# A two-layer attention encoder on one Trainium2 core: the first layer's value products regrouped, and the last gate columns cut unevenly

## The chip, the cores and the metric

The kernel runs on one core of one Trainium2 chip. The metric is the device time of one execution in microseconds (us). Before the change the median of three executions is 668.27 us (667.93 to 668.65).

The engines are named as the profile names them: PE is TensorE (PEld its weight loads), DVE is VectorE, ACT is ScalarE, POOL is GpSimd, SP is SyncE, whose queue issues most DMAs.

## The reference

Two layers over 512 tokens of 1024 features, batch 1. Layer 0 mixes tokens by a two-dimensional neighbourhood attention with 16 heads of 64 channels; layer 1 by a dense latent attention with rotary parts. Cut to what matters here:

```
def mixer_na(xn, w_in, rpb, w_out):                 # layer 0
    q, k, v, z = split(xn @ w_in, 4)                # 1024 columns each
    o = neighbourhood_attention(q, k, v, rpb)       # 16 heads; softmax over an 8 x 16 window
    return (o * silu(z)) @ w_out

def mixer_mla(xn, w_in, q_norm, w_qb, kv_norm, w_kvb, w_out):   # layer 1
    c_q, c_kv, k_rope, z = split(xn @ w_in)
    q, kv = rmsnorm(c_q) @ w_qb, rmsnorm(c_kv) @ w_kvb
    # the rotary part of q and k: x * cos + swapped(x) * sin
    return (attention(q, k, v) * silu(z)) @ w_out

for i in range(2):
    h = x + mixer[i](rmsnorm(x))
    gate = sigmoid(rmsnorm(h) @ ple_w_gate[i])
    x = h + gate * (p[i] @ ple_w_proj[i])
return rmsnorm(x)
```

## The kernel before

**Split products.** Every operand of a large product is held as two float32r tiles, `hi` (a rounded copy) and `lo` (the rest), and a product is three: hi·hi, lo·hi, hi·lo. `load_w` brings a block of weights (`wraw`, 128x1024) in by SP's queue, ACT rounds it to `whi` (L78) and POOL subtracts to `wlo` (L79). Each of the three has a ring of three buffers, so a block can be loaded only when the block three before it has been used up by PE.

**Order.** The kernel is written as a stream of tile operations; a scheduler in the build then sets the order on every engine by what its own timeline takes to be ready. Each engine runs its list strictly in that order. Buffers of a pool are handed out in the order in which the source asks for them. PSUM has eight banks: two named `mm` (projections), two `S` (scores), three `T` (transposed softmax weights), one `O` (a head's output).

**Layer 0's heads** (`na_heads`). Heads go in eight pairs. `values()` makes V of the first eight heads: 96 products of 512 columns into the three `T` banks and the `O` bank at once, ahead of all heads. `project(j)` makes a pair's queries and keys (two groups of 24 products of 512 columns in the `mm` banks). For j = 4 and j = 6 it first makes V of two further pairs (four heads): four groups of 24 products of only 256 columns each, in the `mm` banks. `attend(j)` runs the two heads of a pair; in the source `project(j + 1)` stands ahead of `attend(j)`.

**One head** (`na_head`). Four query quarters. Scores go to the two `S` banks, two quarters in each (L335, L336; 8 products). DVE adds the bias into the tile `ex` and takes the row maximum (L342 for the first quarter, in two pieces, L345 for the others; each with a short read of the accumulator). ACT takes the exponential (L352), DVE the reciprocal of the row sum (L354, once for two quarters), POOL multiplies (L358). PE transposes `ex` block by block into two `T` banks (L369, L371; 7 transposes, the third of the first bank needs the fourth quarter). ACT rounds to `ph` (L89), DVE subtracts to `pl` (L91); PE multiplies by V into the `O` bank (L383; 8 products, the last four need the second `T` bank's `ph` and `pl`). ACT and DVE bring the halves of O together (`half_of`, L193 and L194), POOL multiplies by the gate z (L198). `ex` has two buffers, so the maxima of a head can be written only when the head two before it is transposed.

**Layer 1's start** (`rope`). The rotary part of the queries goes ACT, DVE (shuffle L584, product with cos L585), POOL (product with sin L586, sum L587), ACT (L588), POOL (L589), and by DMA into the query tile `qe` of the first scores.

**The end** (`gate_phase`, `done`). The last output tile's 512 columns of the gate product are made in two groups of 24 products with 256 columns. Per group ACT takes the sigmoid (L480) and DVE applies it (L481, L483). For the first group ACT sums squares (L875) and DVE scales the sum (L876, tile `mn`); for the second DVE does that itself (L871) on top of the first's `mn`. Then POOL takes the root (L882), ACT and DVE scale the row (L886, L883, L885) and two DMAs write it.

Of the kernel before, what the change touches and what calls it, by code (L numbers as in the profile page):

```python
# [14 lines left out]
F32R = mybir.dt.float32r  # L15
AF = mybir.ActivationFunctionType
ALU = mybir.AluOpType
AX = mybir.AxisListType
PSUM = bass.MemoryType.PSUM
P = 128  # L20
S = 512
D = 1024
NT = S // P
KD = D // P
# [15 lines left out]
class Trunk:  # L40
# [172 lines left out]
    def na_heads(self, pool, xT, zs, oT):  # L213
        nc, a = self.nc, self.a
        xh, xl = xT
        X = lambda t, k, kt: t[k // 4][:, k % 4, kt * P:(kt + 1) * P]
        V, A, U = {}, {}, {}

        def values():

            pss = [self.psum(b) for b in ("T", "T", "T", "O")]
            for c in range(4):
                w = self.load_w(a["na_v0"][c], 1024)
                for i, (s, r) in enumerate(((0, 0), (1, 0), (0, 1))):
                    for kt, ps in enumerate(pss):
                        for k in (2 * c, 2 * c + 1):
                            nc.tensor.matmul(ps, X((xh, xl)[s], k, kt), w[r][:, k % 2 * S:(k % 2 + 1) * S],  # L227
                                             start=k == 0 and i == 0, stop=k == KD - 1 and i == 2)
            for g in range(2):
                V[g] = [pool.tile([P, S], F32R, name="vt", tag="vt", bufs=8) for kt in range(NT)]  # L230
            for kt, ps in enumerate(pss):
                for g in range(2):
                    self.v_split(V[g][kt], ps[:, g * 256:(g + 1) * 256])

        def project(j):
            if j in (4, 6):
                g = j // 2
                wv = [self.load_w(a["na_v1"][g - 2, c], 1024) for c in range(2)]
                vts = V[g] = []
                for kt in range(4):  # L240
                    ps = self.psum("mm")
                    W = lambda s, k: wv[k // 4][s][:, (k % 4) * 256:(k % 4 + 1) * 256]
                    t = [(X(xh, k, kt), W(0, k)) for k in range(KD)]
                    t += [(X(xl, k, kt), W(0, k)) for k in range(KD)]
                    t += [(X(xh, k, kt), W(1, k)) for k in range(KD)]
                    self.mms(ps[:, :256], t)
                    vt = pool.tile([P, S], F32R, name="vt", tag="vt", bufs=8)
                    self.v_split(vt, ps[:, :256])
                    vts.append(vt)
            wq = self.load_w(a["na_qk"][j], 1024)  # L250
            psq = self.psum("mm")
            self.proj_T(psq, wq, xT)
            sa = pool.tile([P, S], F32R, name="sa", tag="qs", bufs=4)
            sb = pool.tile([P, S], F32R, name="sb", tag="qs", bufs=4)
            nc.scalar.activation(sa[0:64], psq[0:64], AF.Copy, scale=0.125)
            nc.scalar.activation(sb[64:128], psq[64:128], AF.Copy, scale=0.125)
            nc.vector.scalar_tensor_tensor(sa[64:128], psq[0:64], 0.125, sa[0:64].bitcast(F32),
                                           op0=ALU.mult, op1=ALU.subtract)
            nc.vector.scalar_tensor_tensor(sb[0:64], psq[64:128], 0.125, sb[64:128].bitcast(F32),
                                           op0=ALU.mult, op1=ALU.subtract)  # L260
            s0 = []
            for s in (sa, sb):
                e0 = pool.tile([P, P], F32R, name="s0", tag="s0", bufs=4)
                nc.vector.tensor_copy(e0.rearrange("p (a b) -> p a b", a=2),
                                      win(s, 0, P, 0, [[448, 2], [1, 64]]).bitcast(F32))
                s0.append(e0)
            wk = self.load_w(a["na_qk"][8 + j], 1024)
            psk = self.psum("mm")
            last = self.proj_T(psk, wk, xT)
            da = pool.tile([P, S], F32R, name="da", tag="kd", bufs=4)  # L270
            db = pool.tile([P, S], F32R, name="db", tag="kd", bufs=4)
            la, lb = self.rest_k[j % 2]
            nc.scalar.activation(da[0:64], psk[0:64], AF.Copy)
            nc.scalar.activation(da[64:128], psk[0:64], AF.Copy)
            nc.scalar.activation(db[64:128], psk[64:128], AF.Copy)
            nc.scalar.activation(db[0:64], psk[64:128], AF.Copy)
            nc.vector.tensor_tensor(out=la[0:64], in0=psk[0:64], in1=da[0:64].bitcast(F32), op=ALU.subtract)
            nc.vector.tensor_tensor(out=lb[64:128], in0=psk[64:128], in1=db[64:128].bitcast(F32), op=ALU.subtract)
            A[j] = (sa, sb), s0, (da, db), (la, lb)
            return last  # L280

        def attend(j):
            sq, s0, dk, kl = A.pop(j)
            O = []
            for e in range(2):
                c = (2 * j + e) % 4 * P
                O.append(self.na_head(pool, 2 * j + e, sq[e], s0[e], dk[e], kl[e],
                                      [vt[:, c:c + P] for vt in V[j // 2]]))
            U[j] = self.combine(pool, O[0], O[1], 2 + NLATE)
            if j in zs:  # L290
                self.gated(U[j], zs[j], oT, j)


        self.rest_k = []
        for i in range(2):
            la = pool.tile([P, S], F32R, name=f"la{i}", bufs=1)
            lb = pool.tile([P, S], F32R, name=f"lb{i}", bufs=1)
            nc.gpsimd.memset(la[64:128].bitcast(F32), 0.0)
            nc.gpsimd.memset(lb[0:64].bitcast(F32), 0.0)
            self.rest_k.append((la, lb))  # L300
        values()
        last = project(0)
        for j in range(8):
            if j < 7:
                last = project(j + 1)
            attend(j)
        late = range(8 - NLATE, 8)
        zs.update(self.z_phase(a["na_z"], xT, late, self.last_exp.ins))
        for j in late:
            self.gated(U[j], zs[j], oT, j)  # L310
        return last.ins
# [153 lines left out]
    def gate_phase(self, pool, layer, hnT, rh, res, after):  # L465
        nc, a = self.nc, self.a
        for n in range(2):
            ws = [self.load_w(a["gate"][layer, n, c], 1024, extra=n == 1 or c == 3) for c in range(4)]
            for t in range(NT):
                pe = pool.tile([P, S], F32, name="pe", tag="pe", bufs=3)  # L470
                nc.sync.dma_start(pe, self.pe[layer][t][:, n * S:(n + 1) * S])
                last = layer == 1 and n == 1 and t == NT - 1
                w = S // 2 if last else S
                for o in range(0, S, w):
                    ps = self.psum("mm")[:, :w]
                    L = lambda s, k: hnT[t][:, s * KD + k, :]
                    W = lambda s, k: ws[k // 2][s][:, (k % 2) * S + o:(k % 2) * S + o + w]
                    self.mms(ps, self.by_chunk(L, W))
                    sg = pool.tile([P, S], F32, name="sg", tag="sg", bufs=2)[:, :w]
                    nc.scalar.activation(sg, ps, AF.Sigmoid, scale=rh[t])  # L480
                    nc.vector.tensor_tensor(out=sg, in0=pe[:, o:o + w], in1=sg, op=ALU.mult)  # L481
                    r = res[t][:, n * S + o:n * S + o + w]
                    nc.vector.tensor_tensor(out=r, in0=r, in1=sg, op=ALU.add)  # L483
                    after(t, n, o, w)
# [49 lines left out]
    def mla_heads(self, pool, xT, cT, sets, oT):  # L534


        nc, a = self.nc, self.a
# [6 lines left out]
        R, V, W_, A, PS = {}, {}, {}, {}, {}  # L544
# [31 lines left out]
        def rope(g, a0, a1):  # L576
# [6 lines left out]
            A["r", g] = nc.scalar.activation(xr, psr, AF.Copy)  # L583
            nc.vector.stream_shuffle(sw, xr, swap)  # L584
            nc.vector.tensor_tensor(out=xr, in0=psr, in1=rc_t, op=ALU.mult)  # L585
            nc.gpsimd.tensor_tensor(out=sw, in0=sw, in1=rs_t, op=ALU.mult)  # L586
            nc.gpsimd.tensor_tensor(out=sw, in0=xr, in1=sw, op=ALU.add)  # L587
            nc.scalar.activation(rh, sw, AF.Copy)  # L588
            A["rl", g] = nc.gpsimd.tensor_tensor(out=rl, in0=sw, in1=rh.bitcast(F32), op=ALU.subtract)  # L589
# [321 lines left out]
def layouts(i):  # L911
# [4 lines left out]
    f = {}  # L916
# [9 lines left out]
    def tiles(w, n):  # L926
        k, m = w.shape
        return w.reshape(k // P, P, m // n, n).transpose(2, 1, 0, 3)
# [1 line left out]
    w = i["na_w_in"][0]  # L930
    f["na_qk"] = c(tiles(w[:, :2048], P).reshape(16, P, 1024))
    f["na_z"] = c(tiles(w[:, 3072:], P).reshape(8, P, 1024))
    f["na_v1"] = c(tiles(w[:, 2560:3072], 256).reshape(2, P, 2, 1024).transpose(0, 2, 1, 3))

    def rows(w):
        return c(tiles(w, S).reshape(2, P, 4, 1024).transpose(0, 2, 1, 3))

    f["na_v0"] = c(tiles(w[:, 2048:2560], S).reshape(P, 4, 1024).transpose(1, 0, 2))
    f["na_o"] = rows(i["na_w_out"][0])
    f["mla_o"] = rows(i["mla_w_out"][0])  # L940
    f["gate"] = c(np.stack([rows(i["ple_w_gate"][l]) for l in range(2)]))
# [60 lines left out]
```

## Time and profile before

| what | value |
|---|---|
| median of the runs (lowest, highest) | 668.27 us (667.93, 668.65) |
| the profiled execution: its time, its span | 667.82 us, 666.0 us |
| granted PE clock, mean | 0.997 |
| busy share of the span: PE, PEld, DVE, ACT, POOL | 99%, 84%, 53%, 61%, 59% |
| layer 0's heads (first value product to the last head's output) | about 44 to 243 us of the span |

The profiled execution lies 0.45 us below the median; what lies between its span and its time, 1.8 us, is outside the instructions shown. Busy times come from the hardware profiler's records; matmuls are pipelined and overlap, so their spacing, not their duration, tells how long PE is taken. A row of a group reads: line, engine, operation, out<-in, count, then the busy time in us, the mean duration in ns, and the idle time of the engine before them with what ended it.

### The profile page before, as it was taken

To read this page: it belongs to the slowest core of one execution; us is meant where nothing else is said; L and a number is where in the kernel's file an instruction comes from. 1 tells how busy PE (TensorE), PEld (TensorE's weight loads), DVE (VectorE), ACT (ScalarE), POOL (GpSimd) and SP (SyncE) were. 2 spreads that over 40 slices of the span, in tenths; PEclk is the share of its full clock that TensorE was granted. 3 is DMA by queue.
4 is the path that set the end of the run, shared out by engine and by line. 5 is a ranking of instruction groups with operands and counts; after the bars stand their busy time and mean duration, and the time that the engine had idled before them with its cause. 6 is when DMAs were issued, how large, how long until landed. Compare 5 with 4: busy or idle time off the path is not lost.

```text
span 666.0 us, 9965 instructions
## 1 busy us (share of the span) xinstructions
PE 657.2 (99%) x3467; PEld 560.1 (84%) x3467; DVE 354.3 (53%) x794; ACT 408.7 (61%) x812; POOL 394.8 (59%) x322
## 2 busy tenths in 40 slices
PE   9999999999999999999999999999999999999995
PEld 6888888988988888888899887888888888888885
DVE  6280375736645514544615613888988875145234
ACT  7672586858767742543434635897989887436423
POOL 0395466576575765843044627786969786858411
PEclk9999999999999999999999999999999999999998
DMA  9943222222142136533233334120201222664022
GB/s 324 342 153 136 95 92 94 78 92 95 55 148 76 64 143 252 190 104 138 103 109 103 106 95 156 35 76 24 70 27 64 64 96 110 236 239 159 31 80 94
DMA packets 32385, 79.09 MB, mean 119 GB/s; under 512 B 4176, under 2 KB 8784, under 8 KB 32336
## 3 DMA queue, kind: packets, MB, share of 16 engines
q1 hardware_dynamic: 31904, 77.68, 34.1%
q10 hardware_dynamic: 432, 0.79, 0.3%
q8 instruction: 27, 0.44, 0.3%
q14 instruction: 22, 0.18, 0.1%
HBM read 66.92 MB, written 8.39 MB: 113 GB/s over the span
## 4 chain that ended last, share of the span: by engine, by line
PE 94%; POOL 1%; ACT 1%; DMA 1%; issue 1%; DVE 1%; POOLq 0%; DVEq 0%; ACTq 0%
PE ps_mm L102 48%; PE ps_S L102 12%; PE ps_mm L551 6%; PE ps_T L128 6%; PE ps_O L662 4%; PE ps_T L102 3%; PE ps_O L102 3%; PE ps_T L227 2%; PE ps_O L383 2%; PE ps_mm L173 2%; PE ps_T L371 2%; PE ps_S L336 1%; PE ps_S L335 1%; PE ps_O L227 1%; POOL ex L647 1%
## 5 line engine op out<-in xcount | busy, mean ns | idle before, releaser
L79 POOL TENSOR_TENSOR wlo<-wraw,whi 128x1024 fp32r<-128x1024 f32 (+5 forms) x106 | 208.0, 1980 | 117.7 <-ACT whi L78 90.7
L78 ACT ACTIVATE whi<-wraw 128x1024 fp32r<-128x1024 f32 (+5 forms) x107 | 92.5, 888 | 84.8 <-PE ps_mm L102 18.7
L647 POOL TENSOR_TENSOR ex<-ex,rc 128x512 f32<-128x512 f32 x64 | 66.0, 1042 | 25.6 <-DVE rc L646 18.7
L102 PE MATMUL ps_mm<-whi,hnT 128*128 128x512 f32 (+1 forms) x272 | 70.2, 378 | 0.0
L102 PEld LDWEIGHTS ps_mm<-whi,hnT 128*128 128x128 f32 x272 | 49.3, 188 | 9.3
L645 ACT ACTIVATE ex<-ps_S,mx 128x512 f32<-128x512 f32 x64 | 44.1, 689 | 12.3 <-DVE mx L643 11.1
L643 DVE TENSOR_REDUCE mx<-ps_S 128x1 f32<-128x512 f32 x64 | 43.7, 683 | 8.5 <-PE ps_S L102 7.7
L91 DVE TENSOR_TENSOR pt_lo<-ps_T,pt_hi 128x512 fp32r<-128x512 f32 x64 | 43.2, 682 | 7.7 <-ACT pt_hi L89 7.3
L358 POOL TENSOR_TENSOR ex<-ex,rc 128x128 f32<-128x128 f32 (+1 forms) x64 | 34.3, 565 | 20.8 <-DVE rc L354 20.8
L102 PE MATMUL ps_mm<-xh,whi 128*128 128x512 f32 x152 | 40.8, 399 | 0.0
L102 PE MATMUL ps_mm<-wlo,hnT 128*128 128x512 f32 (+1 forms) x136 | 40.6, 378 | 0.0
L89 ACT ACTIVATE pt_hi<-ps_T 128x512 fp32r<-128x512 f32 x64 | 37.8, 595 | 4.0 <-PE ps_T L128 3.8
L128 PE MATMUL ps_T<-ident,ex 128*128 128x128 f32 x256 | 38.4, 272 | 0.0
L102 PE MATMUL ps_mm<-xl,whi 128*128 128x512 f32 x152 | 38.2, 390 | 0.0
L102 PE MATMUL ps_mm<-xh,wlo 128*128 128x512 f32 x152 | 38.0, 390 | 0.0
L128 PEld LDWEIGHTS ps_T<-ident,ex 128*128 128x128 f32 x256 | 31.5, 140 | 7.7 <-POOL ex L647 0.4
L102 PEld LDWEIGHTS ps_mm<-xl,whi 128*128 128x128 f32 x152 | 28.4, 188 | 5.8
L102 PEld LDWEIGHTS ps_mm<-xh,wlo 128*128 128x128 f32 x152 | 28.3, 188 | 5.8
L112 POOL TENSOR_TENSOR rs<-ss,half 128x1 f32<-128x1 f32 x20 | 12.7, 640 | 34.3 <-DVE ss L111 34.2
L194 DVE TENSOR_TENSOR u<-ps_O,u 64x512 f32<-64x512 f32 x32 | 22.0, 687 | 19.9 <-ACT u L193 19.3
L352 ACT ACTIVATE ex<-ex,mx 128x128 f32<-128x128 f32 (+1 forms) x64 | 30.4, 477 | 1.8 <-DVE mx L342 1.0
L481 DVE TENSOR_TENSOR sg<-pe,sg 128x512 f32<-128x512 f32 (+1 forms) x17 | 12.4, 729 | 35.8 <-ACT sg L480 35.8
(354 smaller groups left out, 1646.7 us busy)
## 6 DMA issues: line engine op xcount, KB each, us to landing
pe<-pe SPq DMA_DIRECT2D x32, 256.0 KB, 2.7
wraw<-na_qk SPq DMA_DIRECT2D x16, 512.0 KB, 3.2
wraw<-gate SPq DMA_DIRECT2D x16, 512.0 KB, 3.2
wraw<-na_v SPq DMA_DIRECT2D x8, 512.0 KB, 3.3
wraw<-na_o SPq DMA_DIRECT2D x8, 512.0 KB, 3.4
wraw<-mla_z SPq DMA_DIRECT2D x8, 512.0 KB, 3.5
wraw<-mla_o SPq DMA_DIRECT2D x8, 512.0 KB, 3.4
wraw<-na_z SPq DMA_DIRECT2D x6, 512.0 KB, 5.5
```

What stands on the lines that cost most here:

```text
L78: nc.scalar.activation(hi[:, c], raw[:, c], AF.Copy)
L79: f = lambda e, c=c: e.tensor_tensor(out=lo[:, c], in0=raw[:, c], in1=hi[:, c].bitcast(F32), op=ALU.subtract)
L89: self.last_copy = nc.scalar.activation(hi, src, AF.Copy, scale=scale)
L91: nc.vector.tensor_tensor(out=lo, in0=src, in1=hi.bitcast(F32), op=ALU.subtract)
L102: last = self.last_mm = nc.tensor.matmul(out, l, r, start=i == 0, stop=i == n - 1)
L128: self.last_mm = self.nc.tensor.transpose(t[:, i * P:(i + 1) * P], b, self.ident)
L352: self.last_exp = nc.scalar.activation(e, e, AF.Exp, scale=-1.0, bias=mx[:, qt:qt + 1], accum_out=sm[:, qt:qt + 1])
L358: nc.gpsimd.tensor_tensor(out=e, in0=e, in1=rc[:, qt:qt + 1].to_broadcast([P, e.shape[1]]), op=ALU.mult)
L551: self.last_mm = nc.tensor.matmul(PS[key], *terms[i], start=i == 0, stop=i == len(terms) - 1)
L643: nc.vector.reduce_max(mx, sp, axis=AX.X, negate=True)
L645: nc.scalar.activation(ex, sp, AF.Exp, bias=mx, accum_out=sm)
L647: nc.gpsimd.tensor_tensor(out=ex, in0=ex, in1=rc.to_broadcast([P, S]), op=ALU.mult)
```

## The change

Four edits:

- `values(h)` now makes V of eight heads for either half, always with 512 columns in the `T` and `O` banks. The first call stands where it stood. The second stands in the source behind `attend(3)` and ahead of `project(5)`.
- `project(4)` and `project(6)` no longer make values. 192 products of 256 columns become 96 of 512. The weights (4 blocks of 128x1024) and the eight splits of V stay as many.
- The last 512 gate columns are made in groups of 384 and 128 instead of 256 and 256.
- For the first group of the rotary queries the product with sin (L586) goes to DVE instead of POOL.

```diff
-        def values():
+        def values(h):
             pss = [self.psum(b) for b in ("T", "T", "T", "O")]
             for c in range(4):
-                w = self.load_w(a["na_v0"][c], 1024)
+                w = self.load_w(a["na_v"][h, c], 1024)
...
-            for g in range(2):
+            for g in (2 * h, 2 * h + 1):
                 V[g] = [pool.tile([P, S], F32R, name="vt", tag="vt", bufs=8) for kt in range(NT)]
...
-            if j in (4, 6):
-                g = j // 2
-                wv = [self.load_w(a["na_v1"][g - 2, c], 1024) for c in range(2)]
-                vts = V[g] = []
-                for kt in range(4):
-                    ps = self.psum("mm")
...
-                    self.mms(ps[:, :256], t)
...
-        values()
+        values(0)
         last = project(0)
         for j in range(8):
             if j < 7:
                 last = project(j + 1)
             attend(j)
+            if j == 3:
+                values(1)
...
-                w = S // 2 if last else S
-                for o in range(0, S, w):
+                for o, w in ((0, 384), (384, 128)) if last else ((0, S),):
...
-            nc.gpsimd.tensor_tensor(out=sw, in0=sw, in1=rs_t, op=ALU.mult)
+            (nc.gpsimd if g else nc.vector).tensor_tensor(out=sw, in0=sw, in1=rs_t, op=ALU.mult)
```

The line numbers of the changed kernel are lower, by 12 at `na_head` (L335, L336 become L323, L324; L345 becomes L333; L354 becomes L342; L369, L371, L383 become L357, L359, L371) and by 13 at the end.

How the built order changes, on PE first. Before, at head 7 (`s_1164` is its first query quarter): between its first two score products and the transposes of head 6 (`ps_T`) stand 24 value products of 256 columns.

```order
L383 MATMUL ps_O<-pl,vt 128x256
L102 MATMUL ps_mm<-wlo,xh_139 128x256
L335 MATMUL ps_S<-db,s_1164 128x256
L336 MATMUL ps_S<-lb_490,s_1164 128x256
L102 MATMUL ps_mm<-whi,xh_138 128x256 x4
L102 MATMUL ps_mm<-whi,xh_139 128x256 x4
L102 MATMUL ps_mm<-whi,xl_140 128x256 x4
L102 MATMUL ps_mm<-whi,xl_141 128x256 x4
L102 MATMUL ps_mm<-wlo,xh_138 128x256 x4
L102 MATMUL ps_mm<-wlo,xh_139 128x256 x4
L369 MATMUL ps_T<-ident,ex 128x2x64
L371 MATMUL ps_T<-ident,ex 128x128 x4
```

Now, on PE, the rows that lead up to the second value products (the last score is head 9's; the `ps_O` rows are head 6's outputs, the four transposes head 7's):

```order
L324 MATMUL ps_S<-lb_486,sb 128x256
L371 MATMUL ps_O<-pl,vt 128x192
L371 MATMUL ps_O<-ph,vt 128x192
L371 MATMUL ps_O<-pl,vt 128x192
L371 MATMUL ps_O<-ph,vt 128x256
L359 MATMUL ps_T<-ident,ex 128x128 x4
L371 MATMUL ps_O<-pl,vt 128x256
L371 MATMUL ps_O<-ph,vt 128x256
L371 MATMUL ps_O<-pl,vt 128x256
L227 MATMUL ps_T<-whi,xh_138 128x512 x2
```

From head 6's first score to this place PE's list holds nothing but work of heads 4 to 9: all 32 scores of heads 6 to 9, 24 output products of heads 4 to 6, and 19 transposes of heads 5 to 7. Behind it the 96 value products follow, with only head 7's outputs in between, and then `project(5)`.

On DVE at the same place, before: the rest of head 6's softmax weights (`pl`) is followed by the maxima of head 8.

```order
L277 TENSOR_TENSOR la_485<-ps_mm,da 64x512
L278 TENSOR_TENSOR lb_486<-ps_mm,db 64x512
L91 TENSOR_TENSOR pl<-ps_T,ph 128x2x192
L354 RECIPROCAL rc<-sm 128x2 x2
L91 TENSOR_TENSOR pl<-ps_T,ph 128x512
L342 ISA ex,mx<-ps_S,bias 64x128
```

Now, on DVE: the last of head 8's maxima (the others stand straight ahead of it), then head 6's two `pl`, then head 9's first maximum.

```order
L333 ISA ex,mx<-ps_S,bias 128x256
L333 ISA mx 128x1
L91 TENSOR_TENSOR pl<-ps_T,ph 128x2x192
L91 TENSOR_TENSOR pl<-ps_T,ph 128x512
L342 RECIPROCAL rc<-sm 128x2 x2
L330 ISA ex,mx<-ps_S,bias 64x128
```

All of head 8's maxima have moved ahead of head 6's `pl`, on which head 6's last outputs wait.

On DVE at the end of the program, before:

```order
L876 TENSOR_SCALAR mn<-ss,mn 128x1
L481 TENSOR_TENSOR sg<-pe,sg 128x256
L483 TENSOR_TENSOR r<-r,sg 128x256
L871 ISA sq,mn<-r,mn 128x256
L871 ISA mn 128x1
L883 SCALAR_TENSOR_TENSOR r<-r,rs,gn 128x256
L885 TENSOR_SCALAR r<-r,rs 128x256
```

and now:

```order
L863 TENSOR_SCALAR mn<-ss,mn 128x1
L468 TENSOR_TENSOR sg<-pe,sg 128x128
L470 TENSOR_TENSOR r<-r,sg 128x128
L858 ISA sq,mn<-r,mn 128x128
L858 ISA mn 128x1
L870 SCALAR_TENSOR_TENSOR r<-r,rs,gn 128x128
L872 TENSOR_SCALAR r<-r,rs 128x384
```

The second group's rows are shorter; they stand behind the first group's `mn`, as before, and that one now covers 384 columns.

More of the change, by code (lines that the diff above doesn't have):

```diff
@@ L232, in values @@
                 for g in range(2):
-                    self.v_split(V[g][kt], ps[:, g * 256:(g + 1) * 256])
+                    self.v_split(V[2 * h + g][kt], ps[:, g * 256:(g + 1) * 256])
         def project(j):
-            if j in (4, 6):
-                g = j // 2
-                wv = [self.load_w(a["na_v1"][g - 2, c], 1024) for c in range(2)]
-                vts = V[g] = []
-                for kt in range(4):
-                    ps = self.psum("mm")
[L242 to L245, printed above, removed]
-                    self.mms(ps[:, :256], t)
-                    vt = pool.tile([P, S], F32R, name="vt", tag="vt", bufs=8)
-                    self.v_split(vt, ps[:, :256])
-                    vts.append(vt)
             wq = self.load_w(a["na_qk"][j], 1024)
@@ L932, in layouts @@
     f["na_z"] = c(tiles(w[:, 3072:], P).reshape(8, P, 1024))
-    f["na_v1"] = c(tiles(w[:, 2560:3072], 256).reshape(2, P, 2, 1024).transpose(0, 2, 1, 3))
     def rows(w):
         return c(tiles(w, S).reshape(2, P, 4, 1024).transpose(0, 2, 1, 3))
-    f["na_v0"] = c(tiles(w[:, 2048:2560], S).reshape(P, 4, 1024).transpose(1, 0, 2))
+    f["na_v"] = rows(w[:, 2048:3072])
     f["na_o"] = rows(i["na_w_out"][0])
```

## The prediction, made before the changed kernel ran

> **What bounds the kernel now.** I read the page's busy times first, then the windows of layer 0's heads, then the chain of waits.
>
> ```profile
> PE 657.2 (99%) x3467; PEld 560.1 (84%) x3467; DVE 354.3 (53%) x794; ACT 408.7 (61%) x812; POOL 394.8 (59%) x322
> PE 94%; POOL 1%; ACT 1%; DMA 1%; issue 1%; DVE 1%; POOLq 0%; DVEq 0%; ACTq 0%
> 120.00:140.00 20.00, 20.00 (x168) 19.78 (x167) 12.96 (x44) 15.39 (x42) 12.32 (x17) 1.00 0.18 58
> 160.00:180.00 20.00, 20.00 (x155) 19.29 (x154) 11.74 (x38) 13.39 (x33) 9.96 (x13) 1.00 0.23 74
> ```
>
> The columns of a window are its length, then busy time and count of PE, PEld, DVE, ACT and POOL, the granted clock, the DMA share. The two windows are those of the value products that the change moves. PE is never idle there and runs at full clock; DVE has about 40% to spare. So a microsecond of PE work taken out is a microsecond gained, and every new wait of PE is lost for good: nothing later has slack to give it back.
>
> Durations overlap, so PE's price is the spacing along the chain (start, length, count):
>
> ```profile
> 134.50 2.88 PE ps_mm L102 x24
> 138.97 10.91 PE ps_mm L102 x48
> 137.49 0.44 PE ps_T L371 x4
> 138.05 0.92 PE ps_O L383 x8
> ```
>
> 24 products of 256 columns take 2.88 us, 0.120 each; 48 of 512 take 10.91, 0.227 each; a transpose takes 0.11; a head's eight output products (half of 192, half of 256 columns) 0.92.
>
> **Part 1, the values' size.** 192 x 0.120 = 23.0 us go, 96 x 0.227 = 21.8 come: **-1.2 us**, all on the path. Loads of weights and the eight splits of V keep their number and size.
>
> **Part 2, the values' place.** What goes is not only PE work but cover: before, the 24-product groups stood between a head's scores and its transposes, while DVE, ACT and POOL did the softmax. In the new order PE runs from head 6's first score to the first value product through 32 scores (3.84 us), 19 transposes, two of them next to free (1.9), and 24 output products (2.8), about 8.6 us, with no projection or value among them: `project(4)` is done, `project(5)`'s weights queue behind the values' in the rings, and the values need the T banks that heads 6 and 7 still use. The softmax work for this stretch, from the groups of layer 0's heads:
>
> ```profile
> L342 DVE CUSTOM_DVE_ANT_0 ex<-ps_S,bias 64x128 f32<-64x128 f32 x32 | 9.2, 288 | 19.6 <-issue 10.0 <-PE ps_S L336 4.7 <-PE ps_T L371 2.4
> L345 DVE CUSTOM_DVE_ANT_0 ex<-ps_S,bias 128x256 f32<-128x256 f32 x48 | 18.7, 422 | 10.6 <-PE ps_S L336 10.0
> L277 DVE TENSOR_TENSOR la<-ps_mm,da 64x512 fp32r<-64x512 f32 x8 | 5.4, 681 | 5.5 <-ACT db L276 5.3
> L278 DVE TENSOR_TENSOR lb<-ps_mm,db 64x512 fp32r<-64x512 f32 x8 | 5.6, 695 | 0.2
> L91 DVE TENSOR_TENSOR pl<-ps_T,ph 128x384 fp32r<-128x384 f32 x16 | 8.8, 552 | 6.1 <-ACT ph L89 6.0
> L91 DVE TENSOR_TENSOR pl<-ps_T,ph 128x512 fp32r<-128x512 f32 x16 | 10.9, 682 | 0.7 <-ACT ph L89 0.7
> L194 DVE TENSOR_TENSOR u<-ps_O,u 64x512 f32<-64x512 f32 x16 | 11.0, 689 | 15.0 <-ACT u L193 14.7
> L354 DVE RECIPROCAL rc<-sm 128x2 f32<-128x2 f32 x32 | 5.0, 161 | 6.4 <-ACT ex L352 6.0
> L352 ACT ACTIVATE ex<-ex,mx 128x256 f32<-128x256 f32 x48 | 24.0, 503 | 0.7 <-DVE mx L345 0.5
> L352 ACT ACTIVATION_READ_ACCUMULATOR ex<-ex,mx 128x1 f32 x64 | 12.2, 191 | 0.0
> L358 POOL TENSOR_TENSOR ex<-ex,rc 128x256 f32<-128x256 f32 x48 | 28.5, 618 | 5.4 <-DVE rc L354 5.4
> ```
>
> DVE's list from head 6's first maximum to its second `pl`, on which the last three outputs of head 6 wait: maxima of heads 6, 7 and 8, 3 x (2 x 0.288 + 3 x 0.422) = 5.5; la, lb 1.4; `pl` of heads 5 and 6, 2 x (0.55 + 0.68) = 2.5; u of heads 4 and 5, 1.4; four reciprocals 0.6. Together 11.4 us, against 7.5 us that PE issues between the same two places. So PE loses at least **3.9 us** there if DVE never waits. It does wait. From the end of `project(4)` (t = 0):
>
> - Head 6's first quarter is readable at 1.05, and its maximum done at 1.65; the second, behind head 4's outputs on PE, is readable at 2.2 and done at 2.6.
> - la, lb and the other two quarters end at 4.85; head 5's first `pl` and head 4's u at 6.1; half of head 7's maxima at 7.1; head 5's second `pl` at 7.8; reciprocal, maximum, reciprocal at 8.5. ACT's exponentials are done by then (about 6.2).
> - POOL's last two products for head 6, 2 x 0.62 behind the first two, end at 10.2; the transposes that need them at 10.8.
> - Only now is head 6's `ex` free for head 8's maxima, which stand ahead of head 6's `pl` on DVE: 1.84 from 11.0 to 12.85, then `pl` 1.2, to 14.1, and PE's last three outputs, to 14.5.
>
> 14.5 less 8.6 is **+5.9 us**. Bounds: 3.9 from below; from above 8.2, if ACT's reading of the accumulator (0.191, in the row above) is paid by each of the 12 exponentials of heads 6 to 8. I take 5.9, which follows the lists. The values themselves should run dense: the weights of their first three blocks are split ahead of the stretch, the fourth's while the third's products run, and the splits of V lie beside `project(5)`'s 10.9 us. Heads 8 and 9 finish their softmax under the values and wait for nothing. POOL's seven `wlo` in a row behind head 9 delay head 10's product, but PE has two projections, 21.8 us, before it needs that.
>
> **Part 3, the rotary product.** Around the first scores of layer 1:
>
> ```profile
> 402.87 2.40 POOL L79 TENSOR_TENSOR wlo<-wraw,whi 128x1024 fp32r<-128x1024 f32 x1 [0.47 <-ACT whi L78]
> 404.08 0.69 DVE L585 TENSOR_TENSOR rh<-ps_mm,rope_c 128x512 f32<-128x512 f32 x1
> 405.22 1.30 POOL L586 TENSOR_TENSOR rl<-rl,rope_s 128x512 f32<-128x512 f32 x1
> 411.96 0.50 PE L102 MATMUL ps_S<-ke,qe 96*128 96x512 f32 x1 [0.33 <-DMA qe<-rl]
> ```
>
> POOL is held by `wlo` until 405.2; on DVE the product can run from 404.8 to 405.5, so the sum starts 1.1 us earlier, and so do the DMAs into `qe`. PE's one visible wait for them is 0.33 us, some 0.5 by the spacing. I take **-0.4**, between 0 (the scores' next wait takes it back) and -0.6.
>
> **Part 4, the last columns.**
>
> ```profile
> 329.24 0.51 PE L102 MATMUL ps_mm<-whi,x1l 128*128 128x384 f32 x2
> 329.59 0.51 PE L102 MATMUL ps_mm<-wlo,x1h 128*128 128x384 f32 x2
> 652.78 0.64 PE L102 MATMUL ps_mm<-whi,hnT 128*128 128x256 f32 x4
> 658.04 0.42 ACT L875 ACTIVATE sq<-r 128x256 f32<-128x256 f32 x1 [0.46 <-DVE r L483]
> 658.59 0.21 DVE L876 TENSOR_SCALAR mn<-ss,mn 128x1 f32<-128x1 f32 x1 [0.64 <-ACT sq L875]
> 658.73 0.47 ACT L480 ACTIVATE sg<-ps_mm,rs 128x256 f32<-128x256 f32 x1 [0.18 <-PE ps_mm L102]
> 659.24 0.42 DVE L481 TENSOR_TENSOR sg<-pe,sg 128x256 f32<-128x256 f32 x1 [0.44 <-ACT sg L480]
> 660.73 0.55 POOL L882 TENSOR_TENSOR rs<-mn,half 128x1 f32<-128x1 f32 x1 [1.38 <-DVE mn L871]
> 661.31 0.72 ACT L886 ACTIVATE r<-r,rs 128x512 f32<-128x512 f32 x1 [2.11 <-POOL rs L882]
> ```
>
> Two products of 384 columns are 0.35 us apart, 0.174 each. No row has a 128-column product of this kind; the transposes, 128 columns with a fresh weight load each, take 0.11. So 24 x 0.174 + 24 x 0.11 = 6.8 against 48 x 0.120 = 5.8: PE ends 1.0 later. Of the work behind it sigmoid, two products and the squares are shorter by about 0.13 each (0.42 for 256 columns, by the 512-column times some 0.29 for 128), 0.5 in all; the last scaling of 512 columns (L886, 0.72) stays. **+0.5 us.** If 128 columns cost half of 256, 0.06 each, PE ends 0.2 earlier, but then the first group's `mn`, 384 columns long, is the gate: its last product, sigmoid, two DVE products and the squares put it 1.0 us later than before (659.8), and the tail is still 0.25 longer. The bounds are -0.3 and +0.6. [...]
>
> **The sum.** Against the profiled execution's 667.82: -1.2 + 5.9 - 0.4 + 0.5 = +4.8, so 672.6; the runs' median lies 0.45 above that execution: **673.1 us**.
>
> **The rivals.**
> - *The waits overlap better than my chain says.* DVE's list alone costs 3.9; without hand-over costs that gives 671.1 us. It lies inside my forecast's own range, 670.5 to 675 (chance of all that 0.70).
> - *The stretch costs PE little*, 1 to 3 us, because heads 6 and 7 are further ahead than I take them to be; for it speaks that PE never waits before, against it that head 6's first score stands behind `project(4)` on PE. 668.2 to 670.2; chance 0.12, half of it within 0.2% of 668.27 (666.9 to 669.6, about what a measurement of this kernel tells from no change).
> - *Faster:* head 6 is no bound at all and only parts 1 and 3 count, with a tail at its better bound: 668.27 - 1.2 - 0.4 - 0.3 = 666.4. It is decided by DVE's list: below 0.5 us of waiting it would be true. PE's idle time in the changed kernel's window of 120 to 155 us would be nil. Chance 0.06.
> - *A second stretch:* head 10's products on POOL behind seven `wlo` come late, or the fourth block of values waits for its `wlo`. Each `wlo` takes 2.40; one too many on the path gives 675.5, two 677.9. Against it: 21.8 us of projections. Chance 0.12.
>
> The range from 669.3 to 676.5 leaves out the faster case, most of the no-change case and the worst of the second stretch. Slower by over 0.2% (above 669.6): 0.70 + 0.12 + 0.05 = 0.87; within: 0.07; faster: 0.06.
>
> **What would show it.** PE's first real idle time in layer 0, some 6 us between head 6's scores and the first `ps_T` value product, ended by DVE and POOL, at about 130 to 146 us of the span; value products 0.227 apart; the wait on `qe<-rl` gone; the last `mn` of the first group near the end later by 1 us. I am wrong if the windows from 120 to 160 show PE as full as before, or if PE waits behind the values as well.

## The result, and the profile after

The changed kernel takes 673.99 us (median, 673.82 to 674.79) against 668.27 us before: ratio 1.0087, 95% interval 1.0074 to 1.0100. The forecast was 673.1 (669.3 to 676.5). The profiled execution of the changed kernel took 674.11 us, its span is 672.3 us.

From the page, the two lines that answer to those shown of before: 96 matmuls fewer, yet PE busy 3.5 us longer, and its share of the chain down from 94% to 92%, DVE's up from 1% to 3%.

```profile
PE 660.7 (98%) x3371; PEld 557.7 (83%) x3371; DVE 358.7 (53%) x795; ACT 407.6 (61%) x812; POOL 394.0 (59%) x321
PE 92%; DVE 3%; POOL 2%; issue 1%; DMA 1%; ACT 1%; POOLq 0%; DVEq 0%; ACTq 0%
```

The windows, with the columns of the prediction's: first the two that were shown of before with the one between them, then four windows of 4 us.

```profile
120.00:140.00 20.00, 17.81 (x108) 15.39 (x108) 12.77 (x43) 16.78 (x43) 12.27 (x13) 1.00 0.28 87
140.00:160.00 20.00, 19.17 (x102) 16.60 (x103) 11.26 (x48) 10.80 (x35) 11.71 (x19) 0.91 0.17 53
160.00:180.00 20.00, 20.00 (x90) 16.58 (x89) 3.86 (x9) 9.75 (x16) 13.63 (x7) 1.00 0.33 106
...
134.00:138.00 4.00, 3.12 (x25) 2.87 (x24) 1.35 (x7) 3.68 (x7) 3.59 (x2) 1.00 0.00 0
138.00:142.00 4.00, 2.37 (x14) 1.91 (x13) 3.91 (x15) 3.15 (x13) 0.02 (x1) 0.89 0.58 179
142.00:146.00 4.00, 3.87 (x22) 3.48 (x21) 2.60 (x13) 2.73 (x9) 3.41 (x7) 0.69 0.20 50
146.00:150.00 4.00, 3.63 (x26) 3.27 (x26) 3.32 (x16) 3.98 (x13) 3.41 (x6) 1.00 0.15 49
```

PE is idle for 3.0 us between 134 and 150 (0.88, 1.63, 0.13 and 0.37), and nowhere else in the heads; from 160 on, under the values, it is full. New is the last but two column: the granted clock falls to 0.89 and 0.69. DVE is the full engine from 138 to 142, with 3.91 of 4.

The timeline of PE, its first score behind `project(4)`, its waits, and the first value products:

```profile
134.36 0.28 PE L323 MATMUL ps_S<-da,s 128*128 128x256 f32 x1
136.19 0.28 PE L324 MATMUL ps_S<-la,sa 128*128 128x256 f32 x1
137.82 0.36 PE L323 MATMUL ps_S<-db,s 128*128 128x256 f32 x1 [0.88 <-DVE mx L333]
139.84 0.39 PE L323 MATMUL ps_S<-db,sb 128*128 128x256 f32 x1 [1.31 <-DVE mx L333]
140.90 0.38 PE L371 MATMUL ps_O<-ph,vt 128*128 128x192 f32 x1 [0.32 <-DVE u L194]
146.70 0.38 PE L323 MATMUL ps_S<-db,s 128*128 128x256 f32 x1 [0.37 <-DVE mx L333]
148.41 0.60 PE L359 MATMUL ps_T<-ident,ex 128*128 128x128 f32 x4
148.77 0.36 PE L371 MATMUL ps_O<-pl,vt 128*128 128x256 f32 x1
149.22 0.62 PE L227 MATMUL ps_T<-whi,xh 128*128 128x512 f32 x2
```

The stretch lasts from 134.36 to 149.22, 14.86 us; the forecast's chain gave 14.5. Behind it the chain of waits shows the values themselves dense, 12 products in 2.72 us, 0.227 each, as forecast:

```profile
149.38 2.72 PE ps_T L227 x12
```

Who holds PE up is read from the lists of DVE and POOL in the same stretch (timeline):

```profile
136.61 0.28 DVE L330 CUSTOM_DVE_ANT_0 ex<-ps_S,bias 64x128 f32<-64x128 f32 x1 [4.44 <-POOL ol L202]
142.35 0.16 DVE L342 RECIPROCAL rc<-sm 128x2 f32<-128x2 f32 x1
145.57 0.28 DVE L330 CUSTOM_DVE_ANT_0 ex<-ps_S,bias 64x128 f32<-64x128 f32 x1 [0.26 <-PE ps_T L359]
147.25 1.15 DVE L91 TENSOR_TENSOR pl<-ps_T,ph 128x384 fp32r<-128x384 f32 x2
...
142.59 4.18 POOL L346 TENSOR_TENSOR ex<-ex,rc 128x128 f32<-128x128 f32 x8 [4.57 <-DVE rc L342]
```

POOL waits 4.57 us for head 6's first reciprocal, which stands on DVE behind head 6's and half of head 7's maxima, la, lb, `pl` and u. Head 8's maxima wait for head 6's transposes (145.57), head 6's `pl` stands behind them and ends at 148.4, and PE's last outputs follow, behind head 7's four transposes (148.41).

### The profile page after: what moved, and what is told of

It is laid out like the page before. It is cut to its first block, busy times and chain, and to the rows that moved or that the text cites. A ratio compares the mean times of both kernels' runs of the same rounds, so it can differ in the third digit from the quotient of the medians.

```text
span 672.3 us, 9778 instructions
## 1 busy us (share of the span) xinstructions
PE 660.7 (98%) x3371; PEld 557.7 (83%) x3371; DVE 358.7 (53%) x795; ACT 407.6 (61%) x812; POOL 394.0 (59%) x321
## 4 chain that ended last, share of the span: by engine, by line
PE 92%; DVE 3%; POOL 2%; issue 1%; DMA 1%; ACT 1%; POOLq 0%; DVEq 0%; ACTq 0%
PE ps_mm L102 42%; PE ps_S L102 13%; PE ps_mm L538 6%; PE ps_T L128 6%; PE ps_T L227 5%; PE ps_O L649 4%; PE ps_T L102 3%; PE ps_O L102 3%; PE ps_O L371 2%; PE ps_O L227 2%; PE ps_mm L173 2%; PE ps_T L359 1%; PE ps_S L323 1%; DVE hg L827 1%; PE ps_S L324 1%
## 5 line engine op out<-in xcount | busy, mean ns | idle before, releaser
L102 PE MATMUL ps_mm<-whi,hnT 128*128 128x512 f32 (+2 forms) x272 | 70.7, 381 | 0.0
L102 PE MATMUL ps_mm<-xh,whi 128*128 128x512 f32 x152 | 42.4, 404 | 0.0
L102 PE MATMUL ps_mm<-wlo,hnT 128*128 128x512 f32 (+2 forms) x136 | 41.0, 382 | 0.0
L468 DVE TENSOR_TENSOR sg<-pe,sg 128x512 f32<-128x512 f32 (+2 forms) x17 | 14.1, 828 | 33.2 <-ACT sg L467 33.2
```

The costliest lines, as they stand in the source:

```text
L102: last = self.last_mm = nc.tensor.matmul(out, l, r, start=i == 0, stop=i == n - 1)
```

## The experiments

Theory: the loss is the missing cover; the stretch is as long as the softmax chain over DVE, ACT and POOL, whatever PE does in it. Rivals: the other edits carry the loss; the T and O banks; the halved clock.

### Each edit alone

The values alone (`values(h)` as in the change, no values in `project`, nothing else):

```diff
-        values()
+        values(0)
...
-            attend(j)
+            attend(j); j == 3 and values(1)
```

> The values' edit alone: the gate's columns and the rotary product stay as before. Theory (the stretch behind project(4) is bound by the softmax chain over DVE, ACT and POOL, +6.3 us by the trace of the changed kernel, less 1.2 for the size): +5.1 us over before, about 673.4, range 672.6 to 674.0; PE idle about 3 us between 134 and 147 us of the span, and the granted clock at half for some 3.4 us there. Rival (the other two edits carry a good part of the loss): below 672.0.

Measured: 673.84 us (673.17 to 674.56), ratio 1.0084 (1.0071 to 1.0098). The stretch is there again, from 134.13 to 148.75, 14.62 us. The values' edit carries the loss; the rival falls.

The columns alone:

```diff
-                w = S // 2 if last else S
-                for o in range(0, S, w):
+                for o, w in ((0, 384), (384, 128)) if last else ((0, S),):
```

> The gate's last columns in 384 and 128, nothing else. Theory (PE ends 1.0 us later, and the 384-column product with gn on POOL holds up the 128-column product with the sigmoid on DVE, 0.93 us where 0.29 was forecast): +0.8 us, 669.1, range 668.6 to 669.5, and that DVE product at 0.9 us again. Rival (my forecast's own term): +0.5 or less, with that product near 0.3 us.

Measured: 669.26 us against 668.18, ratio 1.0014 (1.0005 to 1.0023), +1.1 us. The timeline of this run:

```profile
653.29 0.87 PE L102 MATMUL ps_mm<-whi,hnT 128*128 128x384 f32 x4
657.48 0.56 PE L102 MATMUL ps_mm<-whi,hnT 128*128 128x128 f32 x4
657.87 0.39 PE L102 MATMUL ps_mm<-wlo,hnT 128*128 128x128 f32 x2
...
659.88 0.39 PE L102 MATMUL ps_mm<-wlo,hnT 128*128 128x128 f32 x2
...
660.52 0.99 POOL L879 TENSOR_TENSOR r<-r,gn 128x384 f32<-128x384 f32 x1 [3.20 <-ACT sq L875]
660.73 0.93 DVE L481 TENSOR_TENSOR sg<-pe,sg 128x128 f32<-128x128 f32 x1
661.70 0.29 DVE L483 TENSOR_TENSOR r<-r,sg 128x128 f32<-128x128 f32 x1
```

The 24 products of 384 columns take 4.19 us, 0.175 each; those of 128 are 0.11 apart (22 of them from 657.48 to 659.88). That is PE's part as forecast. But DVE's product with the sigmoid takes 0.93 beside a POOL product, while the next one of the same size takes 0.29.

The next kernel takes that POOL product away (in it DVE scales the last 512 columns with gn at the very end):

```diff
-                            nc.gpsimd.tensor_tensor(out=r[:, c], in0=r[:, c], in1=gn[:, c], op=ALU.mult)
+                            c.start < S and nc.gpsimd.tensor_tensor(out=r[:, c], in0=r[:, c], in1=gn[:, c], op=ALU.mult)
...
-                        nc.vector.scalar_tensor_tensor(r[:, c], r[:, c], rs, gn[:, c], op0=ALU.mult, op1=ALU.mult)
-                        if c.start > S:
-                            nc.vector.tensor_scalar(r[:, S:c.start], r[:, S:c.start], rs, None, op0=ALU.mult)
+                        nc.vector.scalar_tensor_tensor(r[:, S:], r[:, S:], rs, gn[:, S:], op0=ALU.mult, op1=ALU.mult)
```

> The gate's columns in 384 and 128 as in the run of that edit alone, but the product of the first 384 columns with gn is no longer made on POOL beside the second group: DVE does it in its last scaling, over 512 columns. Theory (that POOL product, 0.99 us, holds up DVE's 128-column product with the sigmoid, 0.93 us against 0.29): the DVE product falls to about 0.3 us and the kernel is 0.6 us faster than the edit alone (669.26), 668.7, range 668.4 to 668.9. Rival (the 0.93 us belongs to the first use of a 128-column tile, not to POOL): it stays 0.9 and the time stays at 669.2.

Measured: 668.76 us against 668.33 (ratio 1.0006, 0.9997 to 1.0015). The columns now cost 0.4 instead of 1.1, and the DVE product is short (timeline):

```profile
660.52 0.29 DVE L481 TENSOR_TENSOR sg<-pe,sg 128x128 f32<-128x128 f32 x1
```

So POOL's product held DVE's: 0.64 us, all of what the tail cost beyond the forecast.

The rotary product alone:

```diff
-            nc.gpsimd.tensor_tensor(out=sw, in0=sw, in1=rs_t, op=ALU.mult)
+            (nc.gpsimd if g else nc.vector).tensor_tensor(out=sw, in0=sw, in1=rs_t, op=ALU.mult)
```

> The rotary product of the first group on DVE, nothing else. Theory: -0.3 us (the one wait of PE for qe goes), 668.0, range 667.7 to 668.3; the product on DVE takes about 1.1 us instead of 0.69 if POOL is busy with a wlo beside it. Rival: 0.0, because the next scores wait instead.

Measured: 667.70 us against 668.18, ratio 0.9993 (0.9984 to 1.0002): -0.5 us, not quite clear of no change. Timeline:

```profile
403.11 2.40 POOL L79 TENSOR_TENSOR wlo<-wraw,whi 128x1024 fp32r<-128x1024 f32 x1 [0.47 <-ACT whi L78]
404.94 1.12 DVE L586 TENSOR_TENSOR rl<-rl,rope_s 128x512 f32<-128x512 f32 x1
406.14 1.29 POOL L587 TENSOR_TENSOR rl<-rh,rl 128x512 f32<-128x512 f32 x1 [0.63 <-DVE rl L586]
411.24 0.86 PE L102 MATMUL ps_S<-ke,qe 96*128 96x512 f32 x3
```

The wait between the second and the third score is gone, though the product takes 1.12 on DVE beside POOL's `wlo` and not 0.69. The sum (L587) starts 1.81 us behind the product with cos (L585, 404.33) instead of 2.52 before (404.08 and 406.60): 0.7 earlier.

### Cover put back

Same values, but `project(5)` ahead of them:

```diff
-            if j < 7:
+            if j < 7 and j != 4:
                 last = project(j + 1)
-            attend(j); j == 3 and values(1)
+            attend(j); last = (project(5), values(1))[0] if j == 3 else last
```

> The values' edit with one thing more: project(5) stands in the source ahead of the second values instead of behind it, so its 96 products of 512 columns (21.8 us) lie beside the softmax of heads 6 and 7. Gate's columns and rotary product as before. Theory (the loss is missing cover): the 6.3 us go and the size's gain stays, -1.2 us against before, 667.1, range 666.4 to 668.3; no PE idle time and full clock from 120 to 200 us. Rival 1 (the T and O banks themselves are the trouble, since heads 7 and 8 must leave them first): still +2 us or more, above 670. Rival 2 (the stall moves to heads 8 and 9, which now have no projection ahead of them): idle time of PE behind the values instead, 669 to 671.

Measured: 668.45 us, ratio 1.0003 (0.9994 to 1.0012). The windows where PE waited:

```profile
138.00:142.00 4.00, 4.00 (x21) 3.33 (x20) 3.71 (x11) 3.80 (x11) 0.46 (x2) 1.00 0.52 169
142.00:146.00 4.00, 4.00 (x30) 3.60 (x28) 2.57 (x12) 2.78 (x9) 4.00 (x5) 1.00 0.07 17
```

Full, at full clock, with the same banks and the same V: 5.4 us come back by one move in the source. The move also changes the built order on DVE: head 6's two `pl` now stand ahead of head 8's maxima. The chain isn't shorter for that (timeline):

```profile
148.21 1.16 DVE L91 TENSOR_TENSOR pl<-ps_T,ph 128x384 fp32r<-128x384 f32 x2
```

Head 6's last `pl` ends at 149.37, 14.8 us after its first score (134.55), against 14.0 in the changed kernel; PE has products to do meanwhile. Neither rival shows. The size's gain, though, doesn't come, and the time lies just above the expected range: 0.3 above before instead of 1.2 below. By the spacing of PE's products about 1.0 us goes to short waits, 0.1 to 0.3 each, at 225 and 281 of the span; the rest isn't traced.

With the rotary edit as well:

> The best parts together: second values behind project(5), the rotary product on DVE, gate's columns as before (256 and 256). If the parts add up: 668.45 less 0.48, 668.0, range 667.5 to 668.4, 0.3 us below before and not below the rotary edit alone (667.70). If the parts meet in a better way: 667.2 or less.

Measured: 667.70 us against 668.15, ratio 0.9994 (0.9985 to 1.0002). The parts add up to no more than the rotary edit alone; no version tried is clearly faster than before.

The same values at the changed place, but in the mm banks, in two passes over the weights:

```diff
+            for kts in ((0, 1), (2, 3)):
+                pss = [self.psum("mm") for _ in kts]
+                for c in range(4):
+                    w = self.load_w(a["na_v"][1, c], 1024)
...
```

> The second values with 512 columns at the same place in the source, but into the two mm banks instead of three T banks and the O bank, so in two passes over the weights: four more blocks are loaded, rounded (ACT 0.99 us each) and split (POOL 2.40 each). Theory (cover is all that is lost): head 6's and 7's softmax lies beside value products again, no PE idle time; the size's -1.2 us less what the wider loads cost, 667.0 to 668.6, 667.6 taken. Rival 1 (the splits of the first two banks wait for head 7's outputs, since V has only eight tiles, and hold the mm banks): 1 to 3 us of PE idle time behind the first 48 products, above 669. Rival 2 (POOL, with 9.6 us more of wlo, is late with the softmax): above 670.

Measured: 670.46 us (670.12 to 671.94), ratio 1.0035 (1.0021 to 1.0049). The stretch is full here too, but PE waits behind the values: `project(5)` waits for the splits of V to leave the mm banks (timeline, then windows):

```profile
170.40 2.51 PE L102 MATMUL ps_mm<-xh,whi 128*128 128x512 f32 x8 [2.41 <-DVE vt L91]
...
172.00:175.00 3.00, 3.00 (x9) 2.32 (x8) 0.00 (x0) 0.00 (x0) 1.57 (x2) 0.50 0.71 262
```

The time is rival 1's, but not its mechanism: the wait stands behind the second 48 products, not the first, and head 7's last output had started at 161.92. The splits themselves come late, on ACT at 169.09 behind a `whi` (167.65) and a `ph` (168.62). After the wait the projection's products come at half clock for 3.4 us, 0.43 apart instead of 0.227: some 1.6 us more. Three of the five executions took 670.1 to 670.5 us at a mean clock of 0.997; two, the profiled one among them, took 671.7 and 671.9 at 0.995 and 0.994.

### What bounds the stretch

Three `ex` buffers instead of two:

```diff
-        ex = pool.tile([P, 896], F32, name="ex", tag="ex", bufs=2)
+        ex = pool.tile([P, 896], F32, name="ex", tag="ex", bufs=3)
```

> The values' edit alone with three ex buffers instead of two, so head 8's maxima no longer wait for head 6's transposes; the built order then puts head 9's maxima, 1.84 us, ahead of head 6's second pl on DVE as well. Theory (DVE's list is the bound): DVE runs without the 1.4 us of waits that it has now but has 1.84 us more to do, so 673.8 plus or minus 0.6. Rival (the wait for ex is the bound, as in the last third of my forecast's chain): 1.5 us or more faster than the edit alone, below 672.4.

Measured: 674.47 us, ratio 1.0092 (1.0078 to 1.0106), 0.6 slower than the values alone. The stretch grows to 15.83 us. The rival falls; the theory's range is missed by 0.1 us. The wait for `ex` is not the bound by itself: freed of it, DVE does head 9's maxima first, and its list is longer. What the wait alone costs, with DVE's order kept, isn't shown.

Extra PE work, 12 products of 512 columns ahead of the second values:

```diff
-            attend(j); j == 3 and values(1)
+            attend(j); j == 3 and (self.mms(self.psum("mm"), [(X(xh, i % 8, 0), xh[i % 2][:, i // 2 % 4, :]) for i in range(12)]), values(1))
```

> The values' edit alone plus 12 extra products of 512 columns on PE (2.7 us, from tiles that are there, into an mm bank that nothing reads) ahead of the second values; they land ahead of head 7's scores. Theory A (DVE's list sets the stretch, PE waits there): the extra work costs much less than its 2.7 us, at most +0.8 us over the values' edit alone (673.84), and the granted clock stays full in the stretch. Theory B (half of the loss is the halved clock after the idle time): the time falls below 673.0, since the clock stays up and PE's own work is done sooner. Rival C (PE has no room there at all): +2.7 us, 676.5.

Measured: 677.08 us (676.09 to 678.28), ratio 1.0131 (1.0117 to 1.0144). By the time rival C, but the trace says otherwise: the stretch did not grow, 134.26 to 148.34, 14.08 us with 2.7 us more work in it. The loss lies behind: the extra products changed the built order, so that five outputs of head 7 stand among the values where their `pl` isn't ready, and the clock falls after that wait (windows):

```profile
152.00:155.00 3.00, 1.41 (x8) 0.80 (x7) 2.46 (x12) 2.65 (x10) 0.00 (x0) 1.00 0.00 0
155.00:158.00 3.00, 3.00 (x11) 2.43 (x11) 0.46 (x3) 0.19 (x2) 2.11 (x4) 0.54 0.27 66
```

So as an experiment on the stretch it was confounded. The pair that followed has one order on all engines, with two and with eight extra products, tied behind given scores of heads 6 and 7:

```diff
+            if h == 7: self.filler((3, 5)[half], half)
...
+            with self.tc.issue_after(self.sc.ins):
+                self.mms(self.ft[:, :512], [(A(i), B(i)) for i in range(n)])
```

> The values' edit alone with two extra products of 512 columns (0.45 us) on PE behind head 7's first four scores, where PE waits 1.3 us. It is the base of a pair: the built order of every engine is the same in both, but for the number of extra products (against the values' edit alone, five outputs of head 7 stand earlier among the values). Both theories: PE still waits some 2.5 us in the stretch, the clock is still halved for some 3.4 us; 673.8 to 676, since the values may wait for head 7's outputs as in the run with twelve extra products.

> The other one of the pair: eight extra products, three behind head 6's last score (PE waits 0.9 us there) and five behind head 7's first four (1.3 us), 1.8 us of work put into waits of 2.2 us. Theory A (the chain over DVE, ACT and POOL sets the stretch, the halved clock only fills PE's waiting time): the same time as with two, within 0.5 us. Theory B (the halved clock behind the waits costs by itself, about half of its 3.4 us): 0.8 to 1.7 us faster than with two although PE does 1.4 us more, and the granted clock is full or nearly so from 138 to 146 us. Rival C (the extra products delay the chain): 0.8 us or more slower.

Measured: 675.82 us with two (ratio 1.0115, 1.0102 to 1.0129), 675.45 with eight (1.0114, 1.0099 to 1.0130). Six products more, 1.4 us of PE work, cost nothing. Both lose 1.5 us to the same early outputs of head 7. In the profiled execution with two, the clock stayed full through the whole stretch, against what was expected, and so it did with eight; the pair therefore doesn't price the halved clock, and the table below has to. With two extra products (windows, then that wait in the timeline):

```profile
137.70:141.10 3.40, 2.21 (x12) 1.59 (x13) 3.34 (x11) 2.75 (x10) 0.21 (x1) 1.00 0.54 159
141.10:144.50 3.40, 3.15 (x21) 2.34 (x19) 2.56 (x13) 2.75 (x9) 2.01 (x4) 1.00 0.25 61
...
155.00 0.36 PE L390 MATMUL ps_O<-pl,vt 128*128 128x192 f32 x1 [1.53 <-DVE pl L91]
```

The stretch's length, from the first score behind `project(4)` to the first value product, in the profiled executions:

| kernel | extra PE work | clock in the stretch | stretch |
|---|---|---|---|
| the change | 0 | 0.50 for 3.4 us, else 1.00 | 14.9 us |
| values alone | 0 | 0.75 in 138 to 142, 0.82 in 142 to 146, else 1.00 | 14.6 |
| two extra products | 0.45 | 1.00 | 14.5 |
| eight extra products | 1.8 | 1.00 | 14.5 |
| twelve extra products | 2.7 | 1.00 | 14.1 |

Theory A: with PE's clock low for a part of the stretch, or with up to 2.7 us more work for PE, the stretch stayed within 0.8 us. By these five executions the halved clock cost at most 0.4 there (14.9 and 14.6 against 14.5).

## Why the prediction was right, point by point

| term | forecast | measured | from |
|---|---|---|---|
| values' size | -1.2 | -1.2 | spacing, 96 products at 0.227; no run has it alone |
| stretch | +5.9 | +6.3 | 14.86 less the 8.6 that PE's work takes |
| rotary product | -0.4 | -0.5 | its run alone, 667.70 against 668.18 |
| last columns | +0.5 | +1.1 | their run alone, 669.26 against 668.18 |
| a wait at 292 us | none | +0.35 | spacing of PE's products |
| sum | +4.8 | +6.05 | medians of the runs: +5.7; profiled executions: +6.3 |

- **Part 1** held by the spacing; with cover, however, nothing of the 1.2 was left: 1.0 went to short waits elsewhere, and 0.5 isn't traced.
- **Part 2**, the term that decides, held in size and in cause. One step of its chain failed: I had head 6's first quarter readable at 1.05, when its own products are done. DVE started at 136.61, 2.25 after `project(4)`, 0.14 after the fourth product into that bank (136.19, 0.28 long) was done: the first maximum waited for both quarters of the bank, and the second then for nothing. (The row names POOL's `ol`, but that ended at 135.69; in the kernel with cover DVE starts 0.14 after that product too, at 136.79.) The chain made the 1.2 us good, since later steps were dearer in my list than on the chip: head 6's last `pl` ended at 14.0, against 14.1. The last outputs ended 0.4 later than I said, and there lies the term's error: head 7's four transposes stand ahead of the last three outputs, 0.36 from 148.41 to 148.77. They are in the order shown above the prediction, and its chain left them out.
- I gave the chip's clock no thought. It was 0.50 for 3.4 us in the middle of the stretch, and the forecast survived since PE was not the bound there. That was luck: nothing in the prediction looked for it.
- That the values run dense and heads 8 and 9 wait for nothing held (160 to 180: PE 20.00 of 20).
- **Part 3** held in time, not in its steps: the product on DVE took 1.13 beside `wlo` and not 0.69, so the sum started 0.7 earlier and not 1.1. That was still enough for the wait on `qe<-rl` to go; the run alone (-0.5) isn't clear of no change.
- **Part 4**: PE's 1.0 was right, the relief behind it (-0.5) was not. The step that failed is "sigmoid, two products and the squares are shorter by about 0.13 each": one product was 0.64 longer, for POOL's 384-column product ran beside it. With that product gone the columns cost 0.4, near the forecast's term. The first group's `mn` came 1.4 later, not 1.0, counted from the first product of the last columns.
- **The rivals**: the stretch that costs little and the faster case fall by PE's 3.0 us of idle time and by the run with cover. So does the one in which the waits overlap better, by the stretch's 6.3 against 3.9. The second stretch did not come: PE is full from 160 on. In other kernels PE waited behind or among the values, but for the splits of V or for head 7's `pl`, neither of which the rival named.

The wait at 292 us stands behind a product like the one of Part 4's error. In the changed kernel's timeline a DVE product of two SBUF tiles, 0.69 at 270.35, takes 2.63 beside a `wlo`, and PE's transposes wait behind it:

```profile
289.35 2.63 DVE L827 TENSOR_TENSOR hg<-r,gp 128x512 f32<-128x512 f32 x1
292.78 0.63 PE L128 MATMUL ps_T<-ident,hg 128*128 128x128 f32 x4 [0.18 <-DVE ss L111]
...
289.02 2.40 POOL L79 TENSOR_TENSOR wlo<-wraw,whi 128x1024 fp32r<-128x1024 f32 x1
```

The kernel before has such long products too, without a wait of PE behind them (timeline):

```profile
282.73 2.63 DVE L840 TENSOR_TENSOR hg<-r,gp 128x512 f32<-128x512 f32 x1
```

There two of the four products of this place are longer than 0.7 (2.93, 0.68, 0.69 and 2.63); in the changed kernel, where `wlo` falls at other times, all four are (0.96, 1.96, 2.70 and 2.63). That this makes the difference is read from the traces; no run changes it alone.

## What to carry to other kernels

On an engine that is full, a block of products is also the cover of whatever other engines do meanwhile: before moving one, add up what the slowest helper's list still has to do between the same two places, and compare it with the work of the full engine that is left there. That comparison (11.4 us of DVE against 7.5 of PE, and the hand-overs) gave the stretch within 0.4 us, and putting other work of the same kind into the gap gave it back. Check with filler tied to a fixed place and the built order compared, since a scheduler answers even a few idle products with another order.

## What the runs showed of the hardware

In the changed kernel the granted clock was 0.50 from 141.07 to 144.48, 3.41 us, and 1.00 in the stretches of that length before and behind. PE was partly idle before it. Windows laid on the edges of the slow block:

```profile
137.65:141.07 3.42, 1.62 (x9) 1.24 (x10) 3.36 (x13) 2.90 (x10) 0.37 (x1) 1.00 0.49 156
141.07:144.48 3.41, 3.41 (x17) 3.35 (x17) 2.39 (x13) 2.65 (x9) 1.89 (x4) 0.50 0.28 64
```

PE was busy for 1.62 of the 3.42 us before the block, and no single wait there was longer than 1.31 us (at 139.84). In the other four kernels with such a block the 3.41 us before it were 1.22 (values alone), 1.42 (two passes), 1.82 (twelve extra products) and 2.05 (three `ex` buffers) busy. The busy share alone isn't shown to decide: with three `ex` buffers the 3.41 us before those were 2.03 busy, and no slow block followed. What starts a block isn't shown. Where PE was the bound as the slow block came, the block cost about 1.6 us: in the two-pass kernel by the spacing above, 0.43 instead of 0.227 for 3.4 us, and with twelve extra products, where PE was busy for 3.00 of 3.00 at 0.54, by an estimate from the same spacing. In the stretch of the changed kernel, which is bound by DVE's list and its hand-overs, it cost at most 0.4 by the table.

Some DVE products with both inputs in SBUF that started while a POOL product was running took longer than their like elsewhere: 0.93 against 0.29 for 128 columns (the columns alone, 660.73, beside 0.99 on POOL from 660.52; 0.29 with that product gone), 1.12 against 0.69 (the rotary product alone, 404.94) and 2.63 against 0.69 (the changed kernel, 289.35) for 512, both beside a `wlo` of 2.40. These three ended 0.15, 0.55 and 0.56 us behind POOL's. One that started first was not longer: 0.69 at 306.57 of the changed kernel, with a `wlo` begun at 306.68. Two kinds of DVE products that read PSUM show no such lengthening in the stretch: the maximum of 128x256 takes 0.42 at 137.25 of the changed kernel beside a `wlo`, and 0.42 at 139.01 without; u takes 0.69 at 144.61 beside POOL's products with the reciprocal, and 0.67 at 140.18 without.
